# A first layer and a second layer from 20 products each: the planner ranks the work of ScalarE and VectorE by when TensorE needs it

## The chip, the cores and the metric

The program runs on one core of one Trainium2 chip. The time is the device time of one execution, in microseconds. Before the change three runs took 882.97, 894.66 and 903.51 us, median 894.66 us. A fourth execution, the one that was profiled, took 880.31 us. Its first and last instruction lie 878.5 us apart (its span), so 1.8 us lie outside the span. TensorE's granted clock was 1.000 throughout.

## The reference

```python
batch, m, k, h, n = 16, 512, 768, 3072, 768
def reference(x, w1, b1, w2):
    y = np.matmul(x, w1) + b1
    y = 0.5 * y * (1.0 + erf(y / np.sqrt(2.0)))
    return np.matmul(y, w2).astype(np.float32)
```

This is a two-layer perceptron on 8192 rows: 768 to 3072 columns, bias, GELU, and back to 768 columns. Inputs and output are float32.

## The kernel before

**Number of products.** TensorE multiplies in float16 with float32 sums. Both layers use a bilinear scheme of the Strassen kind, in which 20 products of sums of blocks take the place of 24 products of blocks. The tables `P1_*` and `P2_*` hold the scheme: sums of weight blocks (`WOPS`), sums of data blocks (`XOPS`), the order of the products (`ORD`), and what is done with their results (`OPS`).

**Layer 1 (line 767, and line 655 for the plain part).** The first 512 rows are multiplied plainly (`plain_group`, 24 matmuls for 512 hidden columns), and so are the other rows for the first 512 hidden columns of the first block. The remaining 7680 rows go in five blocks of 1536 rows. Each block goes through six units (one per 512 hidden columns), but for the first block, which has five. A unit has 20 products of three matmuls 128x128 by 512, so 60 matmuls, and there are 29 units.

**Chains.** A unit's 20 products go to five or six chains. A chain is one PSUM bank to which products are added one after another. Between two products of a chain the running sum is read out: the value after the fourth product of chain 3 is itself one of the results. So a product of a chain may start only when those readers have read the bank. The readers are of three kinds: a copy to SBUF (tile `vt`, eight buffers; ScalarE, line 349, or VectorE), an addition or subtraction with an SBUF value (VectorE, lines 342 and 344), and a final result, a GELU with bias on ScalarE (line 513) that reads PSUM or `vt`, writes float16 to SBUF, and is followed by a store to DRAM on SyncE's queue (line 519, tile `gd`). Below, product 16 of a unit is the one with index 16 in `P1_ORD`, `(3, 16, 12)`: the fifth of chain 3. It waits for `('F', [(-1, 0, 3, 3)], 6)`, a GELU that reads PSUM after product 13.

**Layer 2 (line 930).** Sixteen row blocks of 512 rows, each a unit of 20 products of eight matmuls 128x128 by 384. A row block's GELU values come back in three loads of 1 MB each (`ar<-gd`, line 896), VectorE makes their sums (line 344, `ar<-ar` 128x1024), and the results leave by line 945. W2 goes through DRAM as float16 (`w2d`), its sums are made on VectorE during the last block of layer 1.

**The planner.** Nothing is issued while the kernel text is read. Every piece of work is a `Task` in `Sched`, with its cost on each engine that can do it. `Sched.run` simulates the engines with these costs, and emits the instructions in the order that comes out. TensorE's order is fixed by the order of `add`. For the others it chooses at each step, on every engine, between *foreground* tasks (no due time: bank readers, GELUs, casts, stores) and *background* tasks (with a due time: the sums for coming products). Foreground goes by the time at which a task could start, and then by age. A background task whose due time has nearly come (within `URG`) competes with the foreground and wins every tie. On the chip each engine then works off its list strictly in that order, and waits where the chip is later than the plan.

**The start.** SyncE's queue loads the four x tiles of the first 512 rows (line 411), then the first 512 columns of W1 in four pieces (line 434): pieces one and two serve the first two of the four plain tiles, pieces three and four the other two. ScalarE casts them to float16 (VectorE may, but takes such a task only if ScalarE is busy for 0.8 us more), TensorE transposes x (line 496), and the copies out of PSUM (lines 502, 504) follow. The next x rows (`x1`, three loads, line 672) and the other W1 columns go over GpSimd's queue. They are held back by a tiny GpSimd copy (line 666), which reads a value of the fourth cast x tile. `awake` (line 613) issues small dummy matmuls, so that TensorE keeps working while it waits for data.

Of the kernel before, what the change touches and what calls it, by code (L numbers as in the profile page):

```python
# [43 lines left out]
DMA_LAG = 2.0  # L44
WIN = 30.0
URG = 1.0


class Val:
# [40 lines left out]

class Task:
    __slots__ = ("eng", "fn", "nd", "outs", "reads", "alloc", "frees", "due", "key", "end",
                 "deps", "work", "port", "started", "late")


class Sched:
# [14 lines left out]
        self.pe_ideal = 10.0  # L111

    def add(self, eng, fn, reads=(), alloc=None, makes=None, after=(), frees=None, due=None, work=0.0,
            order=(), port=False, late=0.0):
        t = Task()
        t.eng, t.fn, t.alloc, t.due, t.work, t.port, t.late = eng, fn, alloc, due, work, port, late
        t.end = None
        self.key += 1
        t.key = self.key
        t.outs = []  # L120
        t.reads = list(reads)
        t.frees = list(reads) if frees is None else list(frees)
        for v in t.frees:
            v.left += 1
        if makes is None:
            makes = [alloc] if alloc is not None else []
        deps = set(after)
        for v in t.reads:
            deps.update(v.prods)
        for v in makes:  # L130
            v.prods.append(t)
        t.deps = list(deps)
        t.nd = 0
        for d in t.deps + list(order):
            if d.end is None:
                d.outs.append(t)
                t.nd += 1
        self.left += 1
        if "PE" in eng:
            self.pe.append(t)  # L140
            t.due = self.pe_ideal
            self.pe_ideal += eng["PE"]
        elif t.nd == 0:
            self._ready(t)
        return t
# [22 lines left out]
    def run(self):  # L168
        drift = 0.0
        while self.left:  # L170
            best = None
            if self.pp < len(self.pe):
                t = self.pe[self.pp]
                drift = max(self.t["PE"] - t.due, 0.0)
                if t.nd == 0:
                    r = self._start(t, "PE")
                    if r is not None:
                        best = (r, 0, "PE", t)
            for e in ("DVE", "ACT", "POOL", "SP"):
                fg = None  # L180
                bg = None
                now = self.t[e]
                for t in self.avail[e]:
                    r = self._start(t, e)
                    if r is None:
                        continue
                    if t.due is None:
                        if e == "DVE" and "ACT" in t.eng and self.t["ACT"] < r + 0.8:
                            continue
                        c = (r, t.key, t)  # L190
                        if fg is None or c[:2] < fg[:2]:
                            fg = c
                    elif e != "POOL" and r > t.due + drift - URG:
                        c = (r, t.due - 1e9, t)
                        if fg is None or c[:2] < fg[:2]:
                            fg = c
                    elif e == "POOL" or "POOL" not in t.eng or r > t.due + drift - WIN:
                        if e == "POOL" and len(t.eng) > 1 and r + t.eng[e] > t.due + drift - 0.5:
                            continue
                        c = (r > now + 0.2, t.due, t.key, r, t)  # L200
                        if bg is None or c[:3] < bg[:3]:
                            bg = c
                if bg is not None and (fg is None or bg[3] + 0.5 * bg[4].eng[e] <= fg[0]):
                    c = (bg[3], 1, e, bg[4])
                elif fg is not None:
                    c = (fg[0], 1, e, fg[2])
                else:
                    continue
                if best is None or c[0] < best[0]:
                    best = c  # L210
            assert best is not None, "no task can start"
            r, _, e, t = best
            d = t.eng[e]
            if t.alloc is not None and t.alloc.pool is not None:
                t.alloc.slot = t.alloc.pool.take()
            t.fn(e)
            t.started = r
            self.t[e] = r + d
            if t.work:
                s = max(self.q[e], r + d)  # L220
                w = t.work
                for o in self.q:
                    if o != e and self.q[o] > s:
                        both = min(t.work, self.q[o] - s)
                        w += both
                        self.q[o] += both
                self.q[e] = s + w
                t.end = s + w + DMA_LAG
            else:
                t.end = r + d + END[e]  # L230
            if t.port and e in ("DVE", "POOL"):
                self.port = r + d
            t.eng = {e: d}
            if e == "PE":
                self.pp += 1
            else:
                for q in self.avail.values():
                    if t in q:
                        q.remove(t)
            for v in t.frees:  # L240
                v.left -= 1
                v.last = max(v.last, t.end)
                if v.left == 0 and v.pool is not None:
                    v.pool.put(v.last + (PE_LAG if e == "PE" else LAG), v.slot)
            for o in t.outs:
                o.nd -= 1
                if o.nd == 0 and "PE" not in o.eng:
                    self._ready(o)
            self.left -= 1
# [3 lines left out]
def kernel(  # L253
# [254 lines left out]
    gst = Pool([O_GST + 1024 * i for i in range(NGST)])  # L508
    gdone = [[] for _ in range(NU)]

    def finish(src, t, row, sg, frees, queue="SP"):
        g = Val(gst)
        ft = S.add({"ACT": 0.61}, lambda e: nc.scalar.activation(  # L513
            out=a16(g.slot, 512), in_=src[1](), func=ACTF.Gelu,
            bias=b1t[:, t:t + 1], scale=float(sg)), reads=src[0], frees=frees, alloc=g, after=b1done)
        un = row // 512

        def st(e):
# [5 lines left out]
    def unit(ORD, LEN, OPS, n, mm, dur, vp, reads_of, frees_of, out_final):  # L524
# [4 lines left out]
        for k, o in enumerate(OPS):  # L529
            for (sg, kind, a, b) in o[1]:  # L530
                if kind == 0:
                    readers.setdefault((a, b), []).append(k)
        opv = [Val(vp) if o[0] == "C" or o[0] == "A" and o[2] < 0 else Val() for o in OPS]
        optask = {}
        prod = {}
# [22 lines left out]
        def add_op(k):  # L558
# [10 lines left out]
            if kind == "C":  # L569
                optask[k] = S.add({"ACT": act_ps(n), "DVE": dve_ps(n)}, lambda e: scale_copy(  # L570
                    e, vt[:, opv[k].slot:opv[k].slot + n], tap(tms[0]), 1),
                    reads=reads, frees=frees, alloc=opv[k])
            elif kind == "A" and outi < 0:
                op, a, b = signed(tms)
                optask[k] = S.add({"DVE": dve_ps(n)}, lambda e: comb(
                    e, vt[:, opv[k].slot:opv[k].slot + n], op, tap(a), tap(b)), reads=reads, frees=frees, alloc=opv[k])
            else:
                optask[k] = out_final(kind, tms, outi, tap, signed, reads, frees)

        def try_ops():  # L580
            prog = True
# [67 lines left out]
    def plain_tile(u, q, xT, row):  # L649
# [5 lines left out]
                nc.tensor.matmul(out=ps[:, bv.slot, :], lhsT=raw_w1(u, 2 * q + kc // 3)[:, kc % 3, :],  # L655
                                 rhs=xT[0]()[:, kc, :], start=(kc == 0), stop=(kc == KC - 1))
        t = S.add({"PE": 6 * MM1}, mm, reads=[done[0][q], done[1][q]] + xT[1], frees=[raw[0], raw[1]] + xT[2], alloc=bv)
        finish(([bv], lambda: ps[:, bv.slot, :]), u * 4 + q, row, 1, [bv])
        return t

    def plain_group(u, xT, row):
# [2 lines left out]
    xt0 = (lambda: a16(x0T.slot, 3072).rearrange("p (k r) -> p k r", r=512), [x0T], [x0T])  # L664
    x1n = []
    x1g = [S.add({"POOL": 0.07}, lambda e: nc.gpsimd.tensor_copy(
        out=tiny[0:1, 33:34], in_=a16(x0n.slot + 3 * 1536, 1)[0:1, :]), reads=[x0v[3]], after=x0c[6:7])]
    for j in range(3):
        if j:
            w1_load(j, x1g)  # L670
# [7 lines left out]
    w1_ops(0, S.pe_ideal + 5.0)  # L678
    x1done = []
    for j in range(3):  # L680
        awake(12, 60)
        for c in range(4):
            s = 4 * j + c
            pt, dur, ev, bv, dv = transpose_tile(
# [64 lines left out]
    def p1_block(b):  # L749
# [4 lines left out]
        for u in range(6):  # L754
# [13 lines left out]
                                     rhs=xa[:, kt * 512:(kt + 1) * 512], start=(first and kt == 0),  # L768
                                     stop=(kt == 2), skip_group_check=True)

            def out_final(kind, tms, outi, tap, signed, reads, frees, u=u):
                q, j = divmod(outi, 3)
                return finish((reads, lambda: tap(tms[0])), u * 4 + q, r0 + j * 512, tms[0][0], frees)

            def frees_of(i, u=u):
                return [xo[P1_ORD[i][2]][0]] + ([wreg[u][P1_ORD[i][1] // 4]] if b == NBK - 1 else [])
# [47 lines left out]
    for hf in range(2):  # L824
# [13 lines left out]
        nop = 0  # L838

        def due_of():  # L840
            return lastb[0][0].due + 20.0 + hf * 30.0 + nop * 2.0
        for (d, op, a, z) in P2_WOPS:
            va, fa, ra = val[a]
            vb, fb, rb = val[z]
# [42 lines left out]
    for pos, un in enumerate(range(NU)):  # L887
# [43 lines left out]
                                 rhs=a16(w2half[w][j // 4].slot + (j % 4) * W1T, NB),  # L931
                                 start=(first and j == 0), stop=(j == 7), skip_group_check=True)

        def out_final(kind, tms, outi, tap, signed, reads, frees, row=row, pos=pos):
            rt, nh = divmod(outi, 2)
            ov = Val(opool)
            late = glast if pos < 2 else ()
            if len(tms) == 1:
                t = S.add({"ACT": act_ps(NB)}, lambda e: scale_copy(
                    e, a32(ov.slot, NB), tap(tms[0]), tms[0][0]), reads=reads, frees=frees, alloc=ov, after=late)  # L940
            else:
                op, a, b = signed(tms)
                t = S.add({"DVE": dve_ps(NB)}, lambda e: comb(e, a32(ov.slot, NB), op, tap(a), tap(b)),
                          reads=reads, frees=frees, alloc=ov, after=late)
            S.add({"SP": 0.45}, lambda e: nc.sync.dma_start(
                out=of[row + rt * P:row + (rt + 1) * P, nh * NB:(nh + 1) * NB], in_=a32(ov.slot, NB)),
                reads=[ov], work=0.55)
# [37 lines left out]
```

## Time and profile before

| what | value |
|---|---|
| median of three runs | 894.66 us (882.97 to 903.51) |
| profiled execution | 880.31 us, span 878.5 us |
| TensorE busy | 857.3 us, 98% |
| VectorE, ScalarE, GpSimd busy | 639.0, 428.7, 41.4 us |
| VectorE busy from 45 to 455 us (layer 1) | 314.3 us of 410 |
| VectorE busy from 540 to 700 us (layer 2) | 117.8 us of 160 |
| matmuls of line 655, 767, 930 | 216, 1740, 2560 |
| HBM read, written | 102.25 MB, 89.65 MB |

A busy engine in this table is one that has an instruction in work. TensorE's matmuls overlap: a 512-column matmul is shown as 379 ns long, while the next starts about 216 ns after it. So a pause of TensorE shows as idle time only in the part that is over some 163 ns.

### The profile page before, as it was taken

How to read it: one execution, taken by the hardware profiler on the slowest of the kernel's cores; microseconds unless marked ns; L12 is line 12 of the kernel's file. 1: busy time of each engine (PE TensorE's matmuls, PEld its weight loads, DVE VectorE, ACT ScalarE, POOL GpSimd, SP SyncE). 2: the span in 40 equal slices, each digit the busy share in tenths (PEclk: the TensorE clock that was granted, in tenths of full speed). 3: DMA queues.
4: the chain of work that ended last, by engine and by line, in shares of the span. 5: the costliest groups of instructions: out<-in, count | busy, mean ns of one | idle time of the engine just before them, and what ended most of it. 6: DMA issues, size and time to landing. Idle time of an engine off the chain costs nothing.

```text
span 878.5 us, 13706 instructions
## 1 busy us (share of the span) xinstructions
PE 857.3 (98%) x4719; PEld 455.3 (52%) x4719; DVE 639.0 (73%) x1083; ACT 428.7 (49%) x724; POOL 41.4 (5%) x86
## 2 busy tenths in 40 slices
PE   7999999999999999999999999999999999999997
PEld 5544444444444444444446666666666666566664
DVE  3596677579568867888967877777777767677763
ACT  7987777777777777788761122121112211112221
POOL 3110001110110110000000000000000000000000
PEclk9999999999999999999999999999999999999999
DMA  9999547996999597367498555665455565454522
GB/s 280 346 246 213 145 132 176 225 246 168 209 243 215 147 244 191 121 210 239 151 320 327 180 164 161 210 216 167 166 179 169 183 216 183 148 178 163 194 72 72
DMA packets 141369, 171.58 MB, mean 195 GB/s; under 512 B 47708, under 2 KB 132724, under 8 KB 135156
## 3 DMA queue, kind: packets, MB, share of 16 engines
q1 hardware_dynamic: 127872, 146.32, 54.0%
q0 software_dynamic: 13392, 24.38, 14.2%
q8 instruction: 37, 0.61, 0.3%
q14 instruction: 32, 0.26, 0.1%
q10 hardware_dynamic: 36, 0.01, 0.0%
HBM read 102.25 MB, written 89.65 MB: 218 GB/s over the span
## 4 chain that ended last, share of the span: by engine, by line
PE 82%; DVE 7%; DMA 4%; ACT 3%; issue 3%; SPq 1%; ACTq 0%; DVEq 0%
PE ps L930 46%; PE ps L767 29%; PE ps L655 5%; DVE vt L344 4%; DVE ar L344 2%; ACT ar L513 2%; DMA gd<-ar 2%; DMA ar<-gd 2%; DMA ar<-in_x_dram 1%; ACT ar L349 1%; ACT vt L349 0%; PE ps L496 0%; SPq L519 0%; PE ps L613 0%; ACT ar L504 0%
## 5 line engine op out<-in xcount | busy, mean ns | idle before, releaser
L930 PE MATMUL ps<-ar 128*128 128x384 f16 x2560 | 416.3, 326 | 3.7 <-DVE vt L344 2.1
L767 PE MATMUL ps<-ar 128*128 128x512 f16 x1740 | 380.0, 379 | 7.9 <-ACT ar L513 7.2
L930 PEld LDWEIGHTS <-ar 128*128 128x128 f16 x2560 | 250.4, 98 | 169.7 <-issue 2.4
L344 DVE TENSOR_TENSOR ar<-ar 128x1024 f16<-128x1024 f16 (+2 forms) x423 | 278.3, 681 | 28.7 <-ACT ar L349 10.8
L767 PEld LDWEIGHTS <-ar 128*128 128x128 f16 x1740 | 170.1, 98 | 217.3 <-issue 15.2
L349 ACT ACTIVATE vt<-ps 128x512 f32<-128x512 f32 (+1 forms) x227 | 122.8, 545 | 259.1 <-PE ps L930 241.2
L344 DVE TENSOR_TENSOR vt<-vt,ps 128x512 f32<-128x512 f32 (+1 forms) x254 | 163.4, 644 | 85.5 <-ACT vt L349 40.0
L344 DVE TENSOR_TENSOR vt<-ps,vt 128x512 f32<-128x512 f32 (+1 forms) x225 | 144.3, 642 | 77.8 <-PE ps L930 37.5
L513 ACT ACTIVATE ar<-vt,b1t 128x512 f16<-128x512 f32 x232 | 162.2, 717 | 71.2 <-DVE vt L344 61.8
L513 ACT ACTIVATE ar<-ps,b1t 128x512 f16<-128x512 f32 x152 | 102.3, 689 | 12.4 <-PE ps L767 3.9
L349 ACT ACTIVATE ar<-vt 128x384 f32<-128x384 f32 x48 | 25.0, 520 | 98.1 <-DVE vt L344 98.0
L655 PE MATMUL ps<-ar 128*128 128x512 f16 x216 | 47.8, 379 | 2.1 <-ACT ar L504 1.3
L349 ACT ACTIVATE ar<-ar 128x384 f16<-128x384 f16 (+4 forms) x50 | 38.8, 830 | 1.5 <-PE ps L655 0.9
L655 PEld LDWEIGHTS <-ar 128*128 128x128 f16 x216 | 21.0, 98 | 26.8 <-issue 1.3
L342 DVE SCALAR_TENSOR_TENSOR vt<-vt,ps 128x512 f32<-128x512 f32 (+1 forms) x45 | 28.6, 636 | 3.0 <-PE ps L930 0.7
L344 DVE TENSOR_TENSOR ar<-vt 128x384 f32<-128x384 f32 x48 | 26.8, 558 | 1.7
L342 DVE SCALAR_TENSOR_TENSOR ar<-vt,ps 128x384 f32<-128x384 f32 x16 | 8.9, 555 | 21.6 <-PE ps L930 21.6
L368 POOL COPY tiny<-tiny 1x1 f16<-1x1 f16 x32 | 8.1, 252 | 260.0 <-DVE tiny L367 259.9
L702 POOL DMA_DIRECT2D xd<-in_x_dram x24 | 16.4, 684 | 5.3 <-issue 5.3
L613 PE MATMUL ps<-ident 128*128 128x128 f16 x106 | 9.2, 249 | 1.4 <-POOL identf masks.py:197 1.4
L504 ACT COPY ar<-ps 128x768 f16<-128x768 f16 x12 | 9.1, 842 | 0.9 <-PE ps L496 0.9
L344 DVE TENSOR_TENSOR ar<-ps,vt 128x384 f32<-128x384 f32 x16 | 8.9, 557 | 0.5
(28 smaller groups left out, 56.0 us busy)
## 6 DMA issues: line engine op xcount, KB each, us to landing
gd<-ar SPq DMA_DIRECT2D x384, 128.0 KB, 4.1
ar<-gd SPq DMA_DIRECT2D x48, 1024.0 KB, 5.4
out_dram<-ar SPq DMA_DIRECT2D x128, 192.0 KB, 2.0
xd<-in_x_dram POOLq DMA_DIRECT2D x24, 384.0 KB, 6.1
ar<-in_w_dram POOLq DMA_DIRECT2D x10, 768.0 KB, 20.7
w2d<-in_w_dram POOLq DMA_DIRECT2D x8, 576.0 KB, 7.8
ar<-w2d SPq DMA_DIRECT2D x8, 576.0 KB, 5.2
ar<-w2d SPq DMA_DIRECT2D x8, 384.0 KB, 6.8
```

Source lines behind the costliest of these rows:

```text
L342: eng.scalar_tensor_tensor(out=o, in0=a, scalar=-1.0, in1=b, op0=ALU.mult, op1=ALU.subtract)
L344: eng.tensor_tensor(out=o, in0=a, in1=b, op=ALU.add if op == "+" else ALU.subtract)
L349: nc.scalar.activation(out=o, in_=a, func=ACTF.Copy, scale=float(sg))
L368: return S.add({"POOL": 0.07}, lambda e: nc.gpsimd.tensor_copy(out=tiny[0:1, 33:34], in_=tiny[0:1, i:i + 1]), reads=[v])
L504: nc.scalar.copy(out=dst_fn(), in_=i)
L513: ft = S.add({"ACT": 0.61}, lambda e: nc.scalar.activation(out=a16(g.slot, 512), in_=src[1](), func=ACTF.Gelu, bias=b1t[:, t:t + 1], scale ...
L613: nc.tensor.matmul(out=ps[:, v.slot, 0:P], lhsT=ident[:], rhs=ident[:], start=True, stop=True)
L655: nc.tensor.matmul(out=ps[:, bv.slot, :], lhsT=raw_w1(u, 2 * q + kc // 3)[:, kc % 3, :], rhs=xT[0]()[:, kc, :], start=(kc == 0), stop=(kc ...
L702: nc.gpsimd.dma_start(out=o.rearrange("(h r) c -> r h c", h=2), in_=i.rearrange("(h r) c -> r h c", h=2))
L767: nc.tensor.matmul(out=ps[:, bk, :], lhsT=w1_ap(u, w)[:, kt * P:(kt + 1) * P], rhs=xa[:, kt * 512:(kt + 1) * 512], start=(first and kt == ...
L930: nc.tensor.matmul(out=ps[:, bk, 0:NB], lhsT=xa[:, j, :], rhs=a16(w2half[w][j // 4].slot + (j % 4) * W1T, NB), start=(first and j == 0), s ...
```

## The change

Seven edits:

1. Foreground tasks get a `prio`, the number of the product in TensorE's whole list that needs them (`need`, found by going back through `OPS`; a GELU from `vt` has no product behind it, and gets 28 products after its unit's first). Among the tasks that could start within `EPS` = 0.12 us, the one with the lowest number goes first. Before, age decided.
2. An overdue background task ranks as if it were needed `SLK` = 3 products after the one that TensorE is at. Before, it went ahead of all that was ready.
3. Until TensorE's 45th task, VectorE takes a task that ScalarE could do too if ScalarE is busy for 0.1 us more (before 0.8 us).
4. The tiny copy that holds back the x1 and further W1 loads reads a value of the second x tile, not the fourth.
5. The dummy matmuls ahead of the second and third set of x1 transposes go (12 each).
6. The due times of the W2 sums move from 20 + 30 per half + 2 per sum to 4 + 28 per half + 1.8 per sum, in us after the first product of the last block.
7. `finish` and `out_final` hand `prio` on.

```diff
+EPS = 0.12
+SLK = 3
...
                     if t.due is None:
-                        if e == "DVE" and "ACT" in t.eng and self.t["ACT"] < r + 0.8:
+                        if e == "DVE" and "ACT" in t.eng and self.t["ACT"] < r + (0.8 if self.pp > 45 else 0.1):
                             continue
-                        c = (r, t.key, t)
+                        c = (max(r, now + EPS), (t.prio, t.key), t, r)
                         if fg is None or c[:2] < fg[:2]:
                             fg = c
                     elif e != "POOL" and r > t.due + drift - URG:
-                        c = (r, t.due - 1e9, t)
+                        c = (max(r, now + EPS), (self.pp + SLK, t.due), t, r)
                         if fg is None or c[:2] < fg[:2]:
                             fg = c
...
-                if bg is not None and (fg is None or bg[3] + 0.5 * bg[4].eng[e] <= fg[0]):
+                if bg is not None and (fg is None or bg[3] + 0.5 * bg[4].eng[e] <= fg[3]):
                     c = (bg[3], 1, e, bg[4])
                 elif fg is not None:
-                    c = (fg[0], 1, e, fg[2])
+                    c = (fg[3], 1, e, fg[2])
...
+        need = [len(ORD) + 8] * len(OPS)
+        for k in range(len(OPS) - 1, -1, -1):
+            for (sg, kind, a, b) in OPS[k][1]:
+                if kind == 0:
+                    need[k] = min(need[k], at[a, b + 1] if b < LEN[a] - 1 else at[a, b] + 7)
+            for (sg, kind, a, b) in OPS[k][1]:
+                if kind == 1:
+                    need[a] = min(need[a], need[k])
+        base = len(S.pe)
...
-                    reads=reads, frees=frees, alloc=opv[k])
+                    reads=reads, frees=frees, alloc=opv[k], prio=base + need[k])
...
-                optask[k] = out_final(kind, tms, outi, tap, signed, reads, frees)
+                optask[k] = out_final(kind, tms, outi, tap, signed, reads, frees, base + need[k])
...
-        out=tiny[0:1, 33:34], in_=a16(x0n.slot + 3 * 1536, 1)[0:1, :]), reads=[x0v[3]], after=x0c[6:7])]
+        out=tiny[0:1, 33:34], in_=a16(x0n.slot + 1536, 1)[0:1, :]), reads=[x0v[1]])]
...
     for j in range(3):
-        awake(12, 60)
+        if j == 0:
+            awake(12, 60)
...
-            return lastb[0][0].due + 20.0 + hf * 30.0 + nop * 2.0
+            return lastb[0][0].due + 4.0 + hf * 28.0 + nop * 1.8
```

More of the change, by code (lines that the diff above doesn't have):

```diff
@@ L92 @@
     __slots__ = ("eng", "fn", "nd", "outs", "reads", "alloc", "frees", "due", "key", "end",
-                 "deps", "work", "port", "started", "late")
+                 "deps", "work", "port", "started", "late", "prio")
 class Sched:
@@ L113, in add @@
     def add(self, eng, fn, reads=(), alloc=None, makes=None, after=(), frees=None, due=None, work=0.0,
-            order=(), port=False, late=0.0):
+            order=(), port=False, late=0.0, prio=1e9):
         t = Task()
-        t.eng, t.fn, t.alloc, t.due, t.work, t.port, t.late = eng, fn, alloc, due, work, port, late
+        t.eng, t.fn, t.alloc, t.due, t.work, t.port, t.late, t.prio = eng, fn, alloc, due, work, port, late, prio
         t.end = None
@@ L509, with finish @@
     gdone = [[] for _ in range(NU)]
-    def finish(src, t, row, sg, frees, queue="SP"):
+    def finish(src, t, row, sg, frees, prio=0, queue="SP"):
         g = Val(gst)
@@ L514, in finish @@
             out=a16(g.slot, 512), in_=src[1](), func=ACTF.Gelu,
-            bias=b1t[:, t:t + 1], scale=float(sg)), reads=src[0], frees=frees, alloc=g, after=b1done)
+            bias=b1t[:, t:t + 1], scale=float(sg)), reads=src[0], frees=frees, alloc=g, after=b1done, prio=prio)
         un = row // 512
@@ L532, in unit @@
                     readers.setdefault((a, b), []).append(k)
+        at = {}
+        cnt = [0] * NCH
+        for i, (c, w, xx) in enumerate(ORD):
+            at[c, cnt[c]] = i
+            cnt[c] += 1
+        need = [len(ORD) + 8] * len(OPS)
[7 more added lines that the diff above has]
+        base = len(S.pe)
         opv = [Val(vp) if o[0] == "C" or o[0] == "A" and o[2] < 0 else Val() for o in OPS]
@@ L575, in add_op @@
                 optask[k] = S.add({"DVE": dve_ps(n)}, lambda e: comb(
-                    e, vt[:, opv[k].slot:opv[k].slot + n], op, tap(a), tap(b)), reads=reads, frees=frees, alloc=opv[k])
+                    e, vt[:, opv[k].slot:opv[k].slot + n], op, tap(a), tap(b)), reads=reads, frees=frees, alloc=opv[k], prio=base + need[k])
             else:
-                optask[k] = out_final(kind, tms, outi, tap, signed, reads, frees)
+                optask[k] = out_final(kind, tms, outi, tap, signed, reads, frees, base + need[k])
         def try_ops():
@@ L657, in plain_tile @@
         t = S.add({"PE": 6 * MM1}, mm, reads=[done[0][q], done[1][q]] + xT[1], frees=[raw[0], raw[1]] + xT[2], alloc=bv)
-        finish(([bv], lambda: ps[:, bv.slot, :]), u * 4 + q, row, 1, [bv])
+        finish(([bv], lambda: ps[:, bv.slot, :]), u * 4 + q, row, 1, [bv], len(S.pe) + 7)
         return t
@@ L769, in mm, with out_final @@
                                      stop=(kt == 2), skip_group_check=True)
-            def out_final(kind, tms, outi, tap, signed, reads, frees, u=u):
+            def out_final(kind, tms, outi, tap, signed, reads, frees, prio, u=u):
                 q, j = divmod(outi, 3)
-                return finish((reads, lambda: tap(tms[0])), u * 4 + q, r0 + j * 512, tms[0][0], frees)
+                return finish((reads, lambda: tap(tms[0])), u * 4 + q, r0 + j * 512, tms[0][0], frees, prio)
             def frees_of(i, u=u):
@@ L932, in mm, with out_final @@
                                  start=(first and j == 0), stop=(j == 7), skip_group_check=True)
-        def out_final(kind, tms, outi, tap, signed, reads, frees, row=row, pos=pos):
+        def out_final(kind, tms, outi, tap, signed, reads, frees, prio, row=row, pos=pos):
             rt, nh = divmod(outi, 2)
@@ L939, in out_final @@
                 t = S.add({"ACT": act_ps(NB)}, lambda e: scale_copy(
-                    e, a32(ov.slot, NB), tap(tms[0]), tms[0][0]), reads=reads, frees=frees, alloc=ov, after=late)
+                    e, a32(ov.slot, NB), tap(tms[0]), tms[0][0]), reads=reads, frees=frees, alloc=ov, after=late, prio=prio)
             else:
@@ L943, in out_final @@
                 t = S.add({"DVE": dve_ps(NB)}, lambda e: comb(e, a32(ov.slot, NB), op, tap(a), tap(b)),
-                          reads=reads, frees=frees, alloc=ov, after=late)
+                          reads=reads, frees=frees, alloc=ov, after=late, prio=prio)
             S.add({"SP": 0.45}, lambda e: nc.sync.dma_start(
```

## The prediction

> **What bounds the kernel.** I read first the span and the busy times.
>
> ```profile
> span 878.5 us, 13706 instructions
> PE 857.3 (98%) x4719; PEld 455.3 (52%) x4719; DVE 639.0 (73%) x1083; ACT 428.7 (49%) x724; POOL 41.4 (5%) x86
> ```
>
> TensorE bounds it; the change removes no real product. So the most it can win is TensorE's lost time. A 512-column matmul starts about 216 ns after the last one (the chain of work has stretches such as 213 matmuls in 46.30 us). From the starts in the timeline: 12.4 us pass before the first product, the pauses of line 767 sum to 11.9 us, the passage to layer 2 loses 1.7 us, layer 2 2.3 us, and 5.3 us lie after the last matmul's start. Second, who ends the pauses: the waits of TensorE from 45 us to 455 us, then from 455 us on.
>
> ```profile
> PE ps L767 <- ACT ar L513: 7.2, 13, 0.8
> PE ps L767 <- ACT vt L349: 0.4, 1, 0.4
> PE ps L767 <- DVE vt L344: 0.2, 1, 0.2
> ```
>
> ```profile
> PE ps L930 <- DVE vt L344: 2.1, 1, 2.1
> PE ps L930 <- DVE ar L344: 1.5, 1, 1.5
> ```
>
> In layer 1 it is ScalarE's GELU, 13 times. By the overlap each shown pause hides 163 ns: 7.2 + 13 x 0.163 = 9.3 us lost. Nearly all fall at product 16 of a unit (14 of 29 units, 9.5 us with a short one). Third, the timeline of such a place.
>
> ```profile
> 366.99 0.68 DVE L342 SCALAR_TENSOR_TENSOR vt<-vt,ps 128x512 f32<-128x512 f32 x1
> 367.11 1.95 ACT L513 ACTIVATE ar<-vt,b1t 128x512 f16<-128x512 f32 x3 [1.75 <-DVE vt L344]
> ...
> 368.96 1.24 ACT L513 ACTIVATE ar<-ps,b1t 128x512 f16<-128x512 f32 x2
> ...
> 369.68 0.38 PE L767 MATMUL ps<-ar 128*128 128x512 f16 x1 [0.48 <-ACT ar L513]
> ```
>
> Product 13 starts at 367.09 us and ends about 367.8. Its reader, the GELU from PSUM, runs only at 368.96, behind three GELUs from `vt` that no product needs. Product 16 could have started at 369.04 and starts at 369.68: 0.64 us lost.
>
> Fourth, the start, by the chain of work in its first 22 us.
>
> ```profile
> 9.46 0.69 ACT ar L504
> 10.14 1.48 ACT ar L349 x2
> 11.62 0.70 ACT ar L504
> 12.32 0.04 issue
> 12.36 5.34 PE ps L655 x24
> ```
>
> ScalarE does two W1 casts and the last x copy in a row, VectorE being idle.
>
> **Part by part.** Sums are against the profiled execution (880.3 us).
>
> *Ranking (edits 1, 7).* Product 13's GELU now has number 16 of its unit, the others 28. When ScalarE takes the second of the three in the example (367.73), the PSUM one is not quite ready (367.8 plus 0.2 to 0.3 us), so it goes third, ends near 369.0, and the pause shrinks from 0.64 to about 0.05 us. Of 9.5 us at product 16 I take 8 us off (bounds 0, if the plan's clock puts the `vt` GELUs more than 0.12 us earlier, and 9.5). What is late next is the postponed `vt` GELU: it holds one of eight buffers, 0.7 us longer, and SyncE's store of it follows later.
>
> *Overdue sums (edit 2).* A sum 128x1536 holds VectorE 0.95 us, and bank readers (0.69 us) stood behind it. Pauses at products 5, 6, 8 and 12 sum to 2.3 us: I take 0.8 off. Against it stands a sum that is late in its turn. VectorE is idle 23% of layer 1 and 26% of layer 2, so most find room; I add 1.0 us of new pauses (bounds 0 and 6). Layer 2's pause of 2.3 us at 753.8 is a load: VectorE waits 3.33 us for the third load of GELU values, which takes 8.1 us where the others take 4.7 to 6.6. Behind it, two sums and another step stood ahead of product 8's reader; one 0.6 us sum may go behind: 0.6 off (bounds 0 and 2.3).
>
> *W2 sums (edit 6).* From 383 to 455 us they already run in gaps between readers, from 384 us on, as the raw W2 arrives, so an earlier due time moves few. The passage's 1.7 us waits for the third GELU load (issued 447.47, landed 454.4), which these sums don't release: 0 (bounds -1.7 and +2).
>
> *Dummy matmuls (edit 5).* 12 take 0.67 us in the chain, twice: 1.3 off, if x1 is there. Cover is thin now: the second x1 load lands at 26.4, the transposes start at 26.49.
>
> *VectorE shares casts (edit 3).* W1's second piece lands at 3.08 + 7.7 = 10.8 us. With a VectorE cast of some 0.5 us (half of the 128x1536 cast's 0.96) the first product could start at 11.4: 1.0 off, if that landing stays.
>
> *The earlier gate (edit 4)* is the disputed one. The value that the copy reads is now written by the third of four casts (4.39 to 6.15 us), at 5.7. The x1 load is issued near 5.9 instead of 9.22, and its packets come 1.7 us after issue (no packet of that queue before 10.9 us now), at 7.6. Then SyncE's queue is still sending W1's first columns. Four pieces of 384 KB in 1 KB packets are 1536; 1404 packets go on that queue from 7.6 to 12.4 us, so some 1330 of them are W1's. Its rate, undisturbed from 8 to 10 us and beside a filled GpSimd queue from 20 to 24 us:
>
> ```profile
> q1 hardware_dynamic: 764, 0.75, 107.6%
> ```
>
> ```profile
> q0 software_dynamic: 388, 0.61, 81.1%
> q1 hardware_dynamic: 390, 0.36, 33.2%
> ```
>
> That is 382 packets per us alone, 97 beside the other queue, which sends packet for packet. 1330 packets at 97 take 13.7 us: the last piece is sent at 21.3. Now it lands 12.7 - 7.6 = 5.1 us after the same point (the slowest DMA engine counts); 3.9 times that is 20, at 27.6. GpSimd's list stays full throughout: W1's second columns and the next x1 load follow 0.76 us apart. So the third plain tile, which needs pieces three and four, starts between 21.8 and 28.1 with a cast of 0.5, instead of 14.95 (12.36 + 12 x 0.216). Half way is 25.0: 10 us added. The first two tiles need pieces one and two, which land from 13.4 to 19.9, and fit before. The other end is edit 3's, -1.0, if the packets don't meet; the nearest case on record, x1's arrival from 10.9 to 11.9 us, has 28 packets against 168, but that queue was running dry. I take the row in which both queues are filled. The planner would not see it: a load's end is fixed when it is placed, before the later one joins.
>
> The clock is granted in full in every stretch of this trace, and TensorE pauses over 2.2 us nowhere after the first product. [...]
>
> Sum: +10.0 (gate) - 1.3 (dummies) - 8.0 - 0.8 - 0.6 (readers) + 1.0 (late sums) = +0.3: **880.6 us** as a profiled execution. The median shown is 14.4 us above that execution, but all four executions average 890.4, and what sets them apart (loads like the 8.1 us one, I think) stays. So I add half of the 14.4, about 7: **888 us** for a median, no change. Runs of one kernel lie 2% apart here, so 2% (17.9 us) is about what a measurement can tell.
>
> **Rivals.** *The queues don't hurt each other* (chance 0.3): the start wins 1.0 instead of losing 10, one dummy set of 0.67 is all that x1's landing lets go, so 880.3 - 1.0 - 0.7 - 8.0 - 0.8 - 0.6 + 1.0 = 870, and 877 as a median. For it: x1 is itself needed by 17.4. Against it: the two rows above.
>
> *Postponed sums stop TensorE* (0.1, slower): in layer 2 each unit's sums follow their loads closely (in all, VectorE waits 7.8 us for them, nine times). If two readers of 0.55 us go ahead of the sum that the next product needs, 1.1 us are lost in each of 15 units, 16.5 us: 880.6 + 16.5 = 897, 904 as a median. It decides where a sum's lead over its product is under 1.1 us. Against it: two pauses in sixteen units now, and 26% of VectorE idle.
>
> *The order doesn't flip* (0.05): the plan's clock has the `vt` GELUs ready first and the 8 us stay: 888.6, 896 as a median.
>
> The forecast has 0.52; 0.03 is left for the rest. Its own range is the gate's ends and the readers': 872 to 899. The range reaches to the first rival's lower part and the second's centre: 868 to 905. Faster by over 2% (under 876.8) is nearly half of the first rival and a little of the forecast: 0.18. Slower by over 2% (over 912.6) takes both the gate's upper end and late sums: 0.07. Within: 0.75.
>
> **What would show it.** Gate: the first x1 load issued near 6 us, the first W1 pieces landing past 13 us, TensorE idle before its third plain tile; right for the rival if line 655 starts near 11.4 and runs on. Ranking: few waits of line 767 for line 513. Late sums: waits of line 930 for `ar` of line 344. Dummies: transposes right behind matmuls at the second and third sets. I would be wrong most likely by the gate's size, in either direction.

## The result and the profile after

The changed kernel takes 877.4 us (median of 22 runs, 870.84 to 892.61) against 884.82 us for the kernel before (22 runs beside them, 877.88 to 903.51). The ratio is 0.9926, with a 95% interval from 0.9898 to 0.9953. So it is 0.7% faster: within the 2% that the forecast called no change, but clear of noise over many runs. The profiled execution took 874.76 us, 5.6 us less than that of the kernel before.

The first lines of the page of the changed kernel:

```profile
span 873.0 us, 13626 instructions
PE 856.2 (98%) x4695; PEld 454.8 (52%) x4695; DVE 640.2 (73%) x1089; ACT 422.7 (48%) x718; POOL 43.4 (5%) x86
```

TensorE still bounds it. Where it now waits, in layer 1 (line 785 was 767) and then in layer 2 (line 948 was 930), columns as in the prediction:

```profile
PE ps L785 <- ACT vt L351: 1.7, 4, 0.9
PE ps L785 <- DVE vt L346: 1.0, 2, 0.6
PE ps L785 <- ACT ar L515: 0.4, 1, 0.4
```

```profile
PE ps L948 <- DVE vt L346: 1.7, 1, 1.7
```

The 13 waits for a GELU (line 513, now 515) have become one. In their place stand six others, above all for a copy to `vt` (line 351), 2.7 us in sum against 7.2. The passage to layer 2 has no wait at all. The place that the prediction showed, in the same unit, by ScalarE's timeline in the changed kernel:

```profile
365.20 1.33 ACT L515 ACTIVATE ar<-vt,b1t 128x512 f16<-128x512 f32 x2 [1.75 <-DVE vt L346]
366.44 0.67 ACT L515 ACTIVATE ar<-ps,b1t 128x512 f16<-128x512 f32 x1
367.01 0.71 ACT L515 ACTIVATE ar<-vt,b1t 128x512 f16<-128x512 f32 x1
```

Product 13 starts at 365.19 us. The GELU that reads its PSUM bank goes third instead of fourth, as worked out, and product 16 starts at 367.16: three products of 0.647 us later, with 0.03 us lost.

The start, by the chain of work from 10 us on:

```profile
4.16 13.52 DMA ar<-in_w_dram
17.67 0.02 issue
17.70 0.85 ACT ar L351
18.55 0.05 issue
18.59 2.12 PE ps L672 x9
```

The chain now goes through the load of W1's fourth piece, issued at 4.16 us and landed at 17.67 instead of 12.7. TensorE stands still for 3.6 us in the middle of its third plain tile.

| place | before, us | after, us | difference | predicted |
|---|---|---|---|---|
| first plain product | 12.36 | 11.73 | -0.6 | (in the gate's 10) |
| pause in the plain tiles | 0 | 3.6 | +3.6 | +10.0, first product included |
| second and third set of transposes | | | -1.5 | -1.3 |
| together: layer 1's first unit starts | 50.57 | 52.03 | +1.5 | +8.7 |
| pauses at product 16 | 9.5 | 1.0 | -8.4 | -8.0 |
| other pauses of layer 1 | 2.4 | 5.8 | +3.4 | +0.2 |
| passage to layer 2 | 1.7 | 0 | -1.7 | 0 |
| pauses of layer 2 | 2.3 | 1.8 | -0.5 | -0.6 |
| sum | | | -5.7 | +0.3 |

The span went down by 5.6 us, so the table is complete to 0.1 us. (A pause is what the starts of neighbouring matmuls lie further apart than 216 ns with 512 columns or 163 ns with 384, counted from 0.04 us on: in the kernel before 1760 matmuls of 384 columns from 455.13 us on took 286.19 us.)

The ratios below leave out executions over 1.5% slower than their kernel's fastest, the medians don't, and where a kernel was profiled in such a long execution, held up by loads at one or two places, the same products or places are compared, not the spans.

### The profile page after: what moved, and what is told of

Its sections match the earlier page's. It is cut to its first block, busy times and chain, and to the rows that moved or that the text cites. A ratio compares the mean times of both kernels' runs of the same rounds, so it can differ in the third digit from the quotient of the medians.

```text
span 873.0 us, 13626 instructions
## 1 busy us (share of the span) xinstructions
PE 856.2 (98%) x4695; PEld 454.8 (52%) x4695; DVE 640.2 (73%) x1089; ACT 422.7 (48%) x718; POOL 43.4 (5%) x86
## 4 chain that ended last, share of the span: by engine, by line
PE 87%; DMA 5%; DVE 3%; ACT 3%; issue 2%; SPq 1%; DVEq 0%; ACTq 0%
PE ps L948 47%; PE ps L785 37%; PE ps L672 2%; DMA gd<-ar 2%; DVE ar L346 2%; DMA ar<-in_w_dram 2%; ACT ar L515 1%; DVE vt L346 1%; DMA ar<-gd 1%; ACT ar L351 1%; DMA ar<-w2d 1%; ACT ar L506 0%; ACT vt L351 0%; SPq L413 0%; SPq L436 0%
## 5 line engine op out<-in xcount | busy, mean ns | idle before, releaser
L346 DVE TENSOR_TENSOR ar<-ar 128x1024 f16<-128x1024 f16 (+2 forms) x423 | 279.1, 680 | 27.5 <-ACT ar L351 11.3
L785 PEld LDWEIGHTS <-ar 128*128 128x128 f16 x1740 | 169.9, 98 | 212.5 <-issue 10.7
L351 ACT ACTIVATE ar<-ar 128x384 f16<-128x384 f16 (+4 forms) x46 | 35.3, 806 | 9.8 <-DMA ar<-in_w_dram 4.9
L370 POOL COPY tiny<-tiny 1x1 f16<-1x1 f16 x32 | 10.2, 318 | 259.3 <-DVE tiny L369 259.3
L353 DVE CAST ar<-ar 128x384 f16<-128x384 f32 (+2 forms) x7 | 4.6, 663 | 11.5 <-DMA ar<-in_x_dram 5.7
```

Source lines behind the costliest of these rows:

```text
L346: eng.tensor_tensor(out=o, in0=a, in1=b, op=ALU.add if op == "+" else ALU.subtract)
L351: nc.scalar.activation(out=o, in_=a, func=ACTF.Copy, scale=float(sg))
L353: eng.tensor_copy(out=o, in_=a)
L370: return S.add({"POOL": 0.07}, lambda e: nc.gpsimd.tensor_copy(out=tiny[0:1, 33:34], in_=tiny[0:1, i:i + 1]), reads=[v])
L785: nc.tensor.matmul(out=ps[:, bk, :], lhsT=w1_ap(u, w)[:, kt * P:(kt + 1) * P], rhs=xa[:, kt * 512:(kt + 1) * 512], start=(first and kt == ...
```

## The experiments

**What the earlier x1 load costs.** Edit 4 undone, in the changed kernel:

```diff
-        out=tiny[0:1, 33:34], in_=a16(x0n.slot + 1536, 1)[0:1, :]), reads=[x0v[1]])]
+        out=tiny[0:1, 33:34], in_=a16(x0n.slot + 3 * 1536, 1)[0:1, :]), reads=[x0v[3]], after=x0c[6:7])]
```

> The changed kernel with edit 4 undone: x1 waits for the fourth x tile again. Theory A (the early x1 load takes packets from W1's last piece, and this is most of the start's loss): W1's fourth piece lands near 12.7 us instead of 17.7, the third plain tile has no pause (3.6 us in the changed kernel), layer 1's first unit starts 1.5 to 2.5 us earlier (52.0 to about 49.8), the span goes from 873.0 to about 870.8. Theory B (x1 itself is what the start waits for): x1 lands later, the transposes of its first set wait for what the tile no longer waits for, the first unit starts within 0.5 us of 52.0 and the span stays at 873.

Measured: 873.91 us (6 runs), ratio to the kernel before 0.9874 (0.9816 to 0.9932). W1's fourth piece lands at 12.8 us, the plain tiles have no pause, and layer 1's first unit starts at 49.46 us, 2.6 us earlier. So theory A holds for the start. The span did not follow, at 873.0 us: a pause of 3.5 us at product 12 of unit 16 took it back. That is another matter, and the reason for the spread below.

**When x1's packets come.** The same copy reads the first (g1) or the third x tile (g3):

```diff
-        out=tiny[0:1, 33:34], in_=a16(x0n.slot + 1536, 1)[0:1, :]), reads=[x0v[1]])]
+        out=tiny[0:1, 33:34], in_=a16(x0n.slot, 1)[0:1, :]), reads=[x0v[0]])]
```

```diff
+        out=tiny[0:1, 33:34], in_=a16(x0n.slot + 2 * 1536, 1)[0:1, :]), reads=[x0v[2]])]
```

> The changed kernel with the x1 load held back by the first x tile instead of the second: issued near 5.2 us instead of 6.05. In three kernels its first packet came 4.35 to 4.45 us after an issue near 6.05. Theory F (a fixed wait after issue): first packet near 9.6 us, W1's fourth piece lands past 18.4, the third plain tile loses over 4 us. Theory T (the packets come only when W1's queue has come to its end part, whatever the issue): first packet near 10.4 again, loss 0.8 to 5.5 us.

> The changed kernel with the x1 load held back by the third x tile: issued near 7.8 us. Theory F: first packet near 12.2 us, W1's fourth piece lands near 12.8, no loss at the third plain tile. Theory T: first packet between 10.4 and 10.9, as with issues at 6.05 and at 9.22; the fourth piece lands at 13 to 16, loss under 2.5 us.

Each was run once (899.8 us with the first tile, 880.75 us with the third), so only the start is read from them.

| x1 issued, us | first packet, us | delay, us | SyncE queue's packets in the delay past 1.72 us | W1's fourth piece lands, us |
|---|---|---|---|---|
| 5.44 (g1) | 9.83 | 4.39 | 950 | 18.66 |
| 5.99 to 6.31 (six kernels) | 10.37 to 10.70 | 4.35 to 4.40 | 992 to 1012 | 14.7 to 18.4 |
| 8.29 (g3) | 11.00 | 2.71 | 350 | 13.02 |
| 9.22 (before) | 10.91 | 1.69 | 0 | 12.73 |

Neither theory holds over the whole range. F is right for early issues (4.4 us, whatever the time), and wrong for g3. T's thought fits the late ones: in the seven kernels that issue x1 from 8.29 to 9.52 us its first packet comes at 10.82 to 11.15 us. What fits both is a count, with an end. The changed kernel's queues from 7.75 to 10.4 us, that is, from 1.7 us after the issue to x1's first packet:

```profile
q1 hardware_dynamic: 998, 0.99, 107.0%
q0 software_dynamic: 1, 0.00, 0.3%
```

and from 11.4 to 12.4 us:

```profile
q0 software_dynamic: 99, 0.15, 83.0%
q1 hardware_dynamic: 86, 0.08, 30.8%
```

In these 2.65 us 998 packets of SyncE's queue (q1) pass and one of GpSimd's (q0), and only then the two go packet for packet, 99 and 86 in a microsecond. Where W1 is nearly through before that, x1 comes sooner: in g3 after 354 packets of q1 from 10 to 11 us, with some 170 of W1's left (117 to 174 in the seven late kernels), which then went beside x1's. What sets the count, and why the turns that follow are one for one, no run shows. That the count is the cause fits these issue times, but it was not varied by itself: at a steady 382 packets per us, 1000 packets and 2.6 us are the same thing.

**What the ranking is worth.** Edits 1 and 2 undone in the changed kernel:

```diff
-EPS = 0.12
+EPS = 0.0
...
-                        c = (max(r, now + EPS), (t.prio, t.key), t, r)
+                        c = (max(r, now + EPS), (0, t.key), t, r)
...
-                        c = (max(r, now + EPS), (self.pp + SLK, t.due), t, r)
+                        c = (max(r, now + EPS), (-1e9, t.due), t, r)
```

> The changed kernel with edits 1 and 2 undone: foreground by time and age, overdue sums ahead of all that is ready. Theory A (the ranking removes the pauses of layer 1): layer 1's pauses go from 6.8 back to about 11.9 us, those at product 16 from 1.0 to about 9.5 us; if the passage to layer 2 is the ranking's doing too, its 1.7 us come back. Span 878 to 880. Theory B (the pauses went because the start shifted the plan, or by the W2 due times): layer 1's pauses stay near 7 us, span 873 to 874.

And edit 2 alone undone, the last of these three lines:

> The changed kernel with edit 2 alone undone: readers are ranked by product, but an overdue sum goes ahead of them again. Theory A (GELUs on ScalarE are the gain, by edit 1): product 16 stays near 1 us of pauses, and layer 1 within 1.5 us of 6.8. Theory B (readers behind sums on VectorE matter as much): products 5 to 8 and 12 lose 3 us or more over the changed kernel's 4.2, span 876 or more. Theory C (the postponed sums cost something): layer 1's new pauses at products 6, 13 and 15 (2.4 us in all) go, span 870 to 872.

Pauses at product 16, over all 29 units: 9.5 us with both undone, 1.04 us with edit 2 alone undone, 1.0 us in the changed kernel. So edit 1 removes them without edit 2, and theory A of both holds there. The kernel with both undone takes 890.7 us (10 runs), ratio 1.0079 (1.0037 to 1.0121): without the ranking the other edits make the kernel slower than before.

With edit 2 alone undone it takes 893.4 us (4 runs, 879.59 to 895.47), too scattered for a ratio.

The pauses at the other products are larger than any of the theories said: with edit 2 undone, products 5 to 8 and 12 lose 18.4 us, against 4.2 in the changed kernel. Part of that is in units 10 and 16, where slow stores hold the kernel up (below), so this profile doesn't settle theory B. With edit 2 undone, product 8 of unit 25 alone waits 6.2 us, and with both undone 6.7 us. What that is, a quieter kernel shows best (below).

**What the W2 due times do.** Edit 6 undone:

```diff
-            return lastb[0][0].due + 4.0 + hf * 28.0 + nop * 1.8
+            return lastb[0][0].due + 20.0 + hf * 30.0 + nop * 2.0
```

> The changed kernel with edit 6 undone: W2 sums due later again. Theory A (the due times hardly move a sum, and cost the last block's units): the passage to layer 2 stays without a pause, the last block's pauses (2.9 us from unit 25 on in the changed kernel) fall by up to 1.7 us, the span is 871 to 873. Theory B (the due times are what took the passage's 1.7 us): the pause is back, span 874 to 875.

Measured: 883.6 us (10 runs), ratio 0.9916 (0.9866 to 0.9967). The wait ahead of layer 2 is back, from the waits of TensorE between 440 and 470 us:

```profile
PE ps L948 <- DVE ar L346: 3.1, 1, 3.1
```

Theory B holds for the pause. The time can't tell: the ratio lies beside that of the changed kernel, 0.9926. The third GELU load is issued 11.4 us before layer 2's first product here (446.8 us), 7.7 us in the kernel before, and 18.0 us in the changed kernel (432.05), where all three follow each other within a microsecond. In the kernel's text two of the three loads go into the space of the raw W2 (`rawx` hands it to `gset[:2]`), which the W2 sums free. In the changed kernel the first of the three waits for just such a sum, by SyncE's waits from 425 to 448 us, VectorE's timeline and SyncE's:

```profile
SPq L914 <- DVE ar L346: 0.3, 1, 0.3
```

```profile
430.18 0.95 DVE L346 TENSOR_TENSOR ar<-ar 128x1536 f16<-128x1536 f16 x1
```

```profile
431.16 1.27 SPq L914 DMA_DIRECT2D ar<-gd  x3
```

With edit 6 undone the last two W2 sums end at 443.7 and 444.6 us, and the second and third load are issued at 446.0 and 446.8.

**Why the executions of one kernel differ.** The changed kernel once more, and beside it the variant with edit 4 undone and W2's eight casting loads spread:

```diff
+    W2_AT = ((0, 80), (0, 100), (1, 72), (1, 90), (1, 108), (2, 72), (2, 90), (2, 108))
...
-              makes=w2dv, work=4.0, after=[gate([place(1 + i // 4, 60 + 10 * (i % 4))])])
+              makes=w2dv, work=4.0, after=[gate([place(*W2_AT[i])])])
```

> The changed kernel itself once more, beside the others of this call. Its ratio to the kernel before is to repeat 0.9926 within its interval. The start should again lose between 0.8 and 5.5 us at the third plain tile (what four kernels with the early x1 load lost), by the time at which W1's fourth piece lands (14.7 to 18.4 us); the passage to layer 2 should be without a pause.

> The changed kernel with edit 4 undone and, new, the eight casting loads of W2 spread over blocks 0 to 2 (products 80 and 100; 72, 90 and 108; 72, 90 and 108, instead of 60, 70, 80, 90 of blocks 1 and 2). Theory N (what makes executions of one kernel differ is that these loads crowd the GELU stores, whose median time to landing was 5.6 to 11.4 us from 250 to 285 us, so that the eight store buffers run out): stores there land in 2 to 4 us, no pause over 1 us is left in units 10 and 14 to 16, the median is 868 to 871 and the executions lie within 8 us instead of 14 to 25. Theory O (the spread comes from elsewhere): the median stays at 873 to 875, the executions as far apart as before.

The changed kernel repeats: 876.32 us (12 runs, 871.25 to 883.96), ratio 0.9937 (0.9900 to 0.9974). The variant takes **869.48 us**, its six runs lie between 868.74 and 870.45, and its ratio is 0.9841 (0.9807 to 0.9875). It beats both kernels. Its waits in layer 1:

```profile
PE ps L785 <- ACT vt L351: 0.8, 3, 0.3
PE ps L785 <- DVE vt L346: 0.5, 1, 0.5
```

What moved with the W2 loads: the DMA issues from 250 to 285 us, with the median us to landing at the end (`ar<-xd` are the transposing loads of x, on the same SyncE queue as the stores). First the kernel with the ranking undone (a long execution, 902 us), then the variant:

```profile
gd<-ar SPq DMA_DIRECT2D x19, 128.0 KB, 11.3
w2d<-in_w_dram POOLq DMA_DIRECT2D x3, 576.0 KB, 15.2
ar<-xd SPq DMA_TRANSPOSE x2, 20.2
```

```profile
gd<-ar SPq DMA_DIRECT2D x33, 128.0 KB, 3.6
w2d<-in_w_dram POOLq DMA_DIRECT2D x3, 576.0 KB, 7.3
ar<-xd SPq DMA_TRANSPOSE x2, 4.2
```

GELU stores take 11.3 us to land in the one and 3.6 us in the other. There are eight store buffers, and some twelve GELUs in a unit of 13 us: at 11 us each, the buffers run out, ScalarE waits for them, and TensorE for ScalarE. The same two kernels' waits of ScalarE from 170 to 300 us:

```profile
ACT ar L515 <- DMA gd<-ar: 16.0, 10, 9.4
```

```profile
ACT ar L515 <- DMA gd<-ar: 1.7, 3, 0.6
```

In the first, TensorE stands 11.2 us at unit 16, product 5. Such pauses, in units 10 and 14 to 16, come in some executions and not in others.

These two kernels differ in more than the spread. The kernel of the first experiment differs from the variant in the spread alone, and goes the same way: there stores take 7.6 us, the transposing loads 15.2, and ScalarE waits 6.9 us for stores (5.8 us at once). So the spread shortens the stores: by the same view their median is 3.1 to 4.9 us in the five kernels with it, and 5.3 to 11.3 us in the nine without. Whether the W2 loads crowd them directly is not shown. In the five profiles with stores over 9 us between 245 and 290 us, the transposing load issued at 255 to 277 us takes 15 to 20 us; in the other nine it takes 4 to 8 us. It goes ahead of stores on their own queue (in the changed kernel one is issued at 255.68 us, the next stores from 258.73 us on). In the kernels with spread W2 loads it meets them for 2 us at most; without the spread it meets them always, and is slow only sometimes. What decides that is open, and W2 loads, transposing loads and stores were not varied apart.

In time the spread is worth little by itself: 0.9841 against 0.9874 for the first experiment's kernel, with intervals that overlap. What stands out is the range of the six runs, 1.7 us against 13.7.

**Does the spread alone do it?** The kernel before, with `W2_AT` as its only edit:

> The kernel before with one new edit, the spread W2 loads of the faster variant (blocks 0, 1 and 2: products 80 and 100; 72, 90 and 108; 72, 90 and 108). If the W2 loads alone make executions of the kernel before lie 25 us apart, these lie within 5 us, near the best of the kernel before: median 876 to 879. By its own trace it keeps the pauses at product 16 (about 9 us) and the 1.7 us of the passage. If the spread needs the ranked plan, they stay over 10 us apart and the median at 883 to 886.

It does not: 882.02 us (12 runs, 876.79 to 892.31), ratio 0.9985 (0.9949 to 1.0021). The best half lies between 876.8 and 880.2 us, as expected, but the others do not follow. Its profiled execution (span 878.4 us) has store times of 4.5 us from 250 to 285 us, 9.2 us at product 16, and no long pause in layer 1. What holds up its longer executions is in no trace here, so it stays open. The quiet of the variant needs the ranked plan and the spread loads: with the ranking and without the spread (the first experiment) runs lay from 870.14 to 883.81 us, with the spread and without the ranking (below) from 883.6 to 907.97.

**The edits' prices in the quiet variant.** Three kernels, each the variant with one thing put back: edit 4 in, edits 1 and 2 out, edit 6 out.

```diff
+        out=tiny[0:1, 33:34], in_=a16(x0n.slot + 1536, 1)[0:1, :]), reads=[x0v[1]])]
```

```diff
+EPS = 0.0
...
+                        c = (max(r, now + EPS), (0, t.key), t, r)
...
+                        c = (max(r, now + EPS), (-1e9, t.due), t, r)
```

```diff
+            return lastb[0][0].due + 20.0 + hf * 30.0 + nop * 2.0
```

> The changed kernel with the spread W2 loads, the early x1 load kept (so the faster variant plus edit 4). It prices edit 4 where little else varies. Five kernels with the early load lost 0.8 to 5.5 us at the third plain tile, and won nothing back by x1: 871 to 873 against 869.5, executions up to 5 us apart. If x1's earlier landing is worth something, it is 869 or less.

> The faster variant with edits 1 and 2 undone (time and age decide, overdue sums first). By the pauses of undisturbed units (7.0 us with the ranking undone against 2.6 to 3.0, and 9.5 against about 1 at product 16) the ranking is worth 6 to 9 us: 876 to 879. If the gain was the quieter plan and not the order, under 2 us: 869 to 871.

> The faster variant with edit 6 undone (W2 sums due later). If the due times take the passage's pause away, as two kernels without them (1.7 and 3.3 us) and six with them (none) say, a pause of 1.5 to 3.5 us is back before layer 2, the third GELU load is issued 7 to 12 us before layer 2 instead of 18, and the time is 871 to 873. If it was chance, no pause and 869 to 870.

| kernel | median, us | runs | ratio to before | interval |
|---|---|---|---|---|
| variant | 869.48 | 868.74 to 870.45 | 0.9841 | 0.9807 to 0.9875 |
| with the early x1 load | 872.65 | 869.46 to 875.29 | 0.9869 | 0.9826 to 0.9912 |
| with the W2 sums due late | 875.64 | 870.53 to 878.78 | 0.9895 | 0.9845 to 0.9945 |
| without the ranking | 886.6 | 883.6 to 907.97 | 1.0048 | 1.0010 to 1.0085 |

The variant was measured at another time than the three, each beside the kernel before. The early load costs 3 us by the medians, with intervals that overlap; in the traces layer 1 starts 2.1 us later (51.57 against 49.49 us). Late due times bring a wait of 4.0 us ahead of layer 2, and 6 us by the medians, again with intervals that overlap. The ranking is worth more than expected, 17 us. Half of that is product 16, 8.3 us of pauses against 0.3. The rest, in the profiled execution, is nearly all one place, by VectorE's timeline of the kernel without the ranking:

```profile
381.85 8.78 DVE L346 TENSOR_TENSOR ar<-ar 128x1536 f16<-128x1536 f16 x10 [0.39 <-DMA gd<-ar]
390.55 0.68 DVE L346 TENSOR_TENSOR vt<-vt,ps 128x512 f32<-128x512 f32 x1
```

Ten W2 sums in a row, made overdue by edit 6, go ahead of a bank reader, and TensorE waits for it:

```profile
PE ps L785 <- DVE vt L346: 7.0, 1, 7.0
```

It is the 6.2 and 6.7 us pause of the two kernels above in which overdue sums go first. It stands in all three profiles with edit 6 and without edit 2, and in none of the other eleven (0.2 us there at most), the two with neither edit among them. So edit 2 is what makes edit 6 safe; at product 16 it moved nothing.

The windows of the same kernel show a second price of such a wait. The columns are the stretch and its length, the engines' busy time, the granted TensorE clock, DMA share and GB/s:

```profile
387.60:391.50 3.90, 0.19 (x1) 0.00 (x0) 3.90 (x6) 0.49 (x2) 0.00 (x0) 1.00 0.00 0
391.50:398.30 6.80, 3.49 (x9) 1.25 (x9) 5.12 (x8) 2.52 (x4) 0.00 (x0) 0.50 0.60 154
398.30:410.00 11.70, 11.66 (x55) 5.21 (x54) 8.19 (x13) 10.40 (x15) 0.00 (x0) 1.00 0.74 260
```

The clock falls to half within the wait, at 391.5 us, and stays there for 6.8 us. TensorE works again from 394.8 us: in the 3.5 us that are left, 9 matmuls take 3.49 us, 0.39 us each instead of 0.216, by that an estimated 1.5 us more.

## Why the prediction was right, step by step

The sign was open and the size small: 888 us was forecast with 868 to 905, 877.4 us was measured, and no term left its bounds, where it had any. But the sum came near by terms that were wrong in opposite ways, so the nearness is in part luck.

- *Ranking, product 16: right.* 8.0 us forecast, 8.4 us found, by the mechanism shown, and by edit 1 alone (1.04 us left without edit 2).
- *The earlier gate: mechanism right, mis-sized.* The step that was off is "its packets come 1.7 us after issue ... at 7.6". The 1.7 us was read where the other queue was running dry. Behind a filled queue it is 4.4 us, so the packets came at 10.4 to 10.7, with 217 to 377 W1 packets left instead of 1330. These then went packet for packet, as the rows said. The loss at the third plain tile was 3.6 us here and 0.8 to 5.5 us in the kernels with the same gate, against +10.0. The bounds, -1.0 to +13, held it. The rival in which the queues don't hurt each other had nearly the right time (877), and the wrong reason.
- *Clock: no term of the sum.* In the changed kernel it was 1.00 up to 870 us, the pause of 3.6 us at the start included, but in the variant with the early load it stood at half from 17.5 to 21.0 us, one microsecond after a pause of 2.5 us. The trace before has a pause of 2.3 us, not 2.2, with the clock in full.
- *W2 sums: wrong, within the bound of -1.7.* The step "which these sums don't release" fails: the sums free the buffers of two of the three loads (above). With the sums due earlier the third load is issued 10 us earlier against layer 2, and the 1.7 us pause goes (present in four profiles without edit 6, 0.7 to 4.2 us, absent in ten with it). The buffer is not all of it: in the kernel before the second load is issued at 437.72 us, the last W2 sum ends at 438.83, and the third load still comes only at 447.47. Why the plan puts it there was not traced.
- *Other readers and late sums: mis-sized.* -0.8 + 1.0 was forecast; the other pauses of layer 1 grew by 3.4 us, to 5.8 us, and in the variant they are 3.5 us. They lie mostly at products 5 to 8 and 12. That the copies and readers waited for there stand behind the tasks that now go first is likely, and was not traced. Edit 2 isn't a gain by itself there, but a guard against edit 6.
- *Layer 2: right in size, wrong in cause.* The pause at unit 12, product 8, is not a chance delay of one load: it stands at the same place in 13 of 14 profiles, with 1.1 to 2.3 us. Why that load is late each time is open. So it does not explain the differences between executions either; for the ranked plan these go with slow GELU stores, which spreading the W2 loads shortens.
- *Dummy matmuls and casts: right.* -1.5 for -1.3, and the first product 0.6 us earlier (1.0 forecast; VectorE's cast took 0.69 us, not 0.5). The second x1 load landed in time.
- *From the profiled execution to the median: mis-sized.* 7 us were added, half of the 14.4 us between the median of three runs and the profiled execution. Over 22 runs the median lies 4.5 us above the profiled execution in the kernel before and 2.6 us in the changed one. So of the 10.6 us by which 888 was too high, 5.8 lie in the sum and 4.4 in this term.
- *Postponed sums stop TensorE, and the order that doesn't flip:* neither was seen.

## What to carry to other kernels

Rank an engine's work by the first matmul that needs it, not by age: that was worth 8 us here, in the profiled executions. A due time that is moved earlier is safe only if overdue work still stands behind what the next products need. When runs of one kernel differ by 2%, look for large transfers beside small stores with few buffers: spreading eight loads, and not a faster instruction, made the ranked kernel steady (its runs lie 1.7 us apart instead of 13.7).

## What the runs showed of the hardware that was not expected

- With x1's loads issued from 5.44 to 6.31 us, while the other queue was filled, x1's first packet came 4.35 to 4.40 us after the issue in all seven kernels. From 1.72 us after the issue until then, 950 to 1012 packets of the other queue passed. After that the two went packet for packet (99 and 86 in a microsecond of the changed kernel). With the issue at 9.22 us (kernel before) the first packet came after 1.69 us, and in the microsecond from there 168 packets of the other queue passed and 28 of its own.
- The clock fell to half during pauses of TensorE or within 2 us of their end: from 391.5 to 398.3 us in the variant without the ranking (a wait of 7.0 us), from 449.2 to 456.0 us in the variant with the W2 sums due late (a wait of 4.0 us), from 17.5 to 21.0 us in the variant with the early x1 load (a pause of 2.5 us). Over the 14 profiles (mean clock 0.989 to 1.000) such stretches lasted 3.4 to 10.2 us, with pauses of 2.2 to 11.2 us. The pauses of 3.6 us (changed kernel, start) and 2.3 us (kernel before) brought none. What decides it was not shown.
